# Modulation rows in four single buffers, multiplied behind a unit's last tap against a copy in PSUM, and feed-forward vectors loaded with the mixer's

## The chip, the cores and the metric

One core of a Trainium2 chip runs the whole program. The metric is the device time of one execution in microseconds (us); less is better. Engines are named as in the profile: PE (matmuls), PEld (its weight loads), DVE (vector), ACT (scalar), POOL (GpSimd), SP (the queue that issues most transfers).

## The reference, cut to what matters

256 tokens of width 1024 pass through two two-layer networks, one behind the other. The first has no modulation. The second modulates every layer with vectors that depend on the conditioning vector `c` alone:

```python
cond = jax.nn.silu(c)
for l in range(2):
    mod = cond @ ada_w[l] + ada_b[l]                 # 1024 -> 6 * 1024
    sh1, sc1, g1, sh2, sc2, g2 = split(mod, 6)
    h = rms_norm(x, norm1_g[l]) * (1 + sc1) + sh1
    x = x + g1 * (mixers(h) @ w_out[l])
    h = rms_norm(x, norm2_g[l]) * (1 + sc2) + sh2
    u = causal_dwconv(h @ ffn_up[l], ffn_conv[l], 3 taps) + ffn_conv_b[l]
    a, g = split(u, 2)
    x = x + g2 * ((a * silu(g)) @ ffn_down[l])
```

The feed-forward blocks of the first network are `(silu(h Wg) * (h Wu)) Wd`, without taps. All four feed-forward blocks have 2816 hidden columns.

## The kernel before, in words

The program runs eight stages: delta-rule mixer (g), feed-forward (f0), latent attention (a), feed-forward (f1), mixer (m0), feed-forward (f2), mixer (m1), feed-forward (f3). Every matmul with a weight is made of three products of high and low parts, so each weight chunk of 512 KB is loaded by SP (`weights`, L458), cast by ACT to its high part (L464), and its low part is made by DVE (L469) or POOL (L467), as a string per stage says. Chunks lie in seven or eight buffers, so this work runs ahead of PE.

A feed-forward block goes through 22 units of 128 hidden columns. Units 0 and 1 come out of `first_units`, token half by token half, with two accumulators of the pool `pa` (four PSUM banks, tag "acc"). From unit 2 on, `mm3_a` fills a `ps_gu` tile (four buffers). The element work of a unit in f0 and f1 is a SiLU on ACT (L735), a product on DVE (L736), a cast on ACT (L737) and a difference on POOL (L738). In f2 and f3 it is longer: ACT scales by the third tap (L2229) and DVE adds the two other taps, for both halves (L2231, four instructions), then SiLU (L2233), product (L2234, POOL), cast and difference. `proj_out` then multiplies by the down weights, chunk by chunk, into four `ps_o` tiles of the pool `pa`: for each chunk first token half 0, then token half 1.

The modulation is worked out beside f0, f1 and f2, as a matrix-vector product on DVE. `ada_cond` (L1363) broadcasts `c` to 128 partitions and takes its SiLU. The transposed modulation weights come in 48 pieces of 1 MB, each two rows of 1024 values per partition. `ada_load` (L1371) issues a piece from ACT's queue into one of two buffers `ada_raw`; `ada_step` (L1381) takes the piece held, loads the next one, and multiplies both rows with `ada_cond`, each in one DVE instruction that also sums it up (L1394). A block does 16 pieces: `ada_step` is called ahead of the element work of every odd unit (11 times) and in the down projection at chunks 1, 5, 9, 13, 17 (`ada_every`). f3 has none. The normed rows `xn` of the block's start lie in the same two buffers, each taking a whole 2 x 1024 buffer for one row of 1024.

The taps and their bias in f2 and f3 (`f2s`, 176 values per partition) are loaded by SP at the start of the block (L2204), among the first weight chunks. `mix2` loads its own vectors (`lay`, L1428) behind the last weight load of the block before.

The order of the instructions on each engine is made at build time by a list scheduler: it takes the code in the order written as priority, simulates the engines, and gives each engine the first instruction that it finds ready. On the chip each engine then keeps that order. `issue_after(ins)` forbids that an instruction of the same engine is put ahead of `ins`.

Of the kernel before, what the change touches and what calls it, by code (L numbers as in the profile page):

```python
# [20 lines left out]
D = 1024  # L21
# [358 lines left out]
class Prog:  # L380
    def __init__(self, ctx, tc, ap):
# [18 lines left out]
        self.ada_held = None  # L400
        self.behind = None
# [240 lines left out]
    def proj_steps(self, x, act, wap, nk, gate=None, order=None, each=None, last=None, out=None, hold=None):  # L642
        nc = self.nc
        tiles = lambda t: [a[:, k] for a in (t if isinstance(t, list) else [t]) for k in range(a.shape[1])]
# [63 lines left out]
    def ffn1(self, x, i):  # L708
        nc = self.nc
        with ExitStack() as st:  # L710
# [3 lines left out]
            xn = [fp.tile([128, 2, D], F32, name="xn", tag="ada_raw", bufs=2)[:, 0] for _ in range(2)]  # L714
# [9 lines left out]
            for m in range(NFF):  # L724
                if m < 2:
                    ps = first[m]
                else:
                    ps = self.pm.tile([128, 2, S], F32, name="ps_gu", tag="mm")
                    for j in range(2):
                        w = self.weights(self.ap[f"f_gu{i}"][2 * m + j], CW)  # L730
                        self.mm3_a(ps[:, j, :], w, KD, 128, 0, 128, hl)
                if m % 2:
                    self.ada_step(fp)
                t = fp.tile([128, S], F32, name="gu_t", tag="gu_t", bufs=2)
                nc.scalar.activation(t, ps[:, 0, :], AF.Silu)  # L735
                nc.vector.tensor_tensor(t, t, ps[:, 1, :], op=ALU.mult)  # L736
                nc.scalar.copy(ah[:, m, :], t)  # L737
                nc.gpsimd.tensor_tensor(al[:, m, :], t, ah[:, m, :].bitcast(F32), op=ALU.subtract)  # L738
# [624 lines left out]
    def ada_cond(self, pool):  # L1363

        nc = self.nc
        c = pool.tile([128, D], F32, name="ada_c", tag="ada_raw", bufs=2)
        self.cond = pool.tile([128, D], F32, name="ada_cond")
        nc.scalar.dma_start(c, self.ap["c"].partition_broadcast(128))
        nc.scalar.activation(self.cond, c, AF.Silu)

    def ada_load(self, pool):  # L1371

        if not self.ada_todo:
            return
        l, c = self.ada_todo.pop(0)
        raw = pool.tile([128, 2, D], F32, name="ada_raw", tag="ada_raw", bufs=2)
        with self.tc.issue_after(self.last_copy.ins):
            self.nc.scalar.dma_start(raw, self.ap[f"ada{l}"][c])
        self.ada_held = l, c, raw

    def ada_step(self, pool, last=False):  # L1381
# [7 lines left out]
        if c == 0:  # L1389
            self.mods[l] = self.xp.tile([128, 48], F32, name=f"mod{l}", tag="mod", bufs=2)  # L1390
        mod = self.mods[l]
        for j in range(2):
            i = 2 * c + j
            nc.vector.tensor_tensor_reduce(raw[:, j], raw[:, j], self.cond, 1.0, 0.0, op0=ALU.mult, op1=ALU.add, accum_out=mod[:, i : i + 1])  # L1394
        if c == 23:
            nc.vector.tensor_tensor(mod, mod, self.col(f"adab{l}", 0, 48), op=ALU.add)
# [3 lines left out]
    def mod_rows(self, l, pool):  # L1400

        nc = self.nc
        mod = self.mods[l]
# [20 lines left out]
    def mix2(self, x, l):  # L1424
        nc, tc, ap = self.nc, self.tc, self.ap
        self.lay = self.xp.tile([128, LAYER.n], F32, name=f"lay{l}", tag="lay")
        with tc.issue_after(self.last_raw.ins):
            nc.sync.dma_start(self.lay, ap[f"layer{l}"])  # L1428
        with ExitStack() as st:
# [768 lines left out]
    def ffn2(self, x, l, out):  # L2198
        nc, tc, ap = self.nc, self.tc, self.ap
        with tc.tile_pool(name=f"ffc{l}", bufs=1, reuse_waits="tile") as fp, ExitStack() as st:  # L2200
            self.psum(st)
            xn = [fp.tile([128, 2, D], F32, name="xn", tag="ada_raw", bufs=2)[:, 0] for _ in range(2)]
            sm = fp.tile([128, FFN2.n], F32, name="f2s")
            nc.sync.dma_start(sm, ap[f"ffn2_{l}"])  # L2204
# [8 lines left out]
            for m in range(NFF):  # L2213
# [10 lines left out]
                if m % 2:  # L2224
                    self.ada_step(fp)
                u = fp.tile([128, 2, S], F32, name="gu_u", tag="gu_u", bufs=2)
                for j in (1, 0):
                    q = NFF * j + m
                    nc.scalar.activation(u[:, j], ps[:, j], AF.Identity, scale=cw[:, 3 * q + 2 : 3 * q + 3], bias=cb[:, q : q + 1])  # L2229
                    for d in (1, 2):  # L2230
                        nc.vector.scalar_tensor_tensor(u[:, j, d:], ps[:, j, : S - d], cw[:, 3 * q + 2 - d : 3 * q + 3 - d], u[:, j, d:], op0=ALU.mult, op1=ALU.add)  # L2231
# [45 lines left out]
```

## Time and profile before

| | us |
|---|---|
| median of 3 runs | 1560.41 |
| lowest, highest | 1558.67, 1565.21 |
| the profiled execution, its own time | 1568.4 |
| span of the profiled execution (first to last instruction) | 1566.7 |
| PE busy | 1458.5 (93%) |
| DVE busy | 1114.1 (71%) |
| ACT busy | 811.6 (52%) |
| POOL busy | 662.0 (42%) |

The span is cut by its stages. The four feed-forward blocks are alike in what PE does, so they can be laid side by side: the start (first normed rows and the two first units), the stretch of the other twenty units, and the down projection. What PE waits for in a stretch is shown by its waits; PEclk is the clock that TensorE was granted, as a share of full speed.

### The profile page before, as it was taken

What the parts mean: (1) busy time and instruction counts of PE and PEld (TensorE: products, weight loads), DVE (VectorE), ACT (ScalarE), POOL (GpSimd) and SP (SyncE); (2) the same over time, 40 slices, a digit from 0 to 9 for tenths busy, and PEclk for the clock granted to TensorE, in tenths of its full rate; (3) what the DMA queues carried; (4) which work ended last, traced back from release to release, by engine and by line L of the source; (5) the groups of instructions that cost most, each with busy time, mean ns of one, the idle gap of its engine ahead of it and who ended that gap; (6) DMA issues with size and microseconds to landing.
All of it is one profiled execution on the core that took longest, in us unless ns stands there. A gap on an engine that the chain in (4) does not pass through costs nothing. (4 is left out here: it accounts for less than half of the span.)

```text
span 1566.7 us, 25783 instructions
## 1 busy us (share of the span) xinstructions
PE 1458.5 (93%) x9586; PEld 1287.5 (82%) x9586; DVE 1114.1 (71%) x2350; ACT 811.6 (52%) x1476; POOL 662.0 (42%) x435
## 2 busy tenths in 40 slices
PE   5999989899999899999998989898999898899998
PEld 4998878699987787999887766898988676689987
DVE  3588668778675576888477587788966868766652
ACT  4676545544543564454355664555545465466651
POOL 3577623246452431533136322465534612236530
PEclk9999999999999999999999999999999999899999
DMA  4756622677883455898544325677764432465551
GB/s 159 232 165 188 187 69 66 209 288 282 297 312 107 152 176 188 304 329 315 178 131 133 108 68 168 226 273 264 265 235 142 129 108 68 142 213 186 191 188 39
DMA packets 103246, 292.96 MB, mean 187 GB/s; under 512 B 28072, under 2 KB 37968, under 8 KB 96976
## 3 DMA queue, kind: packets, MB, share of 16 engines
q1 hardware_dynamic: 93872, 237.12, 46.0%
q10 hardware_dynamic: 8896, 53.14, 9.3%
q8 instruction: 75, 1.23, 0.3%
q0 software_dynamic: 352, 1.06, 0.2%
q14 instruction: 51, 0.42, 0.1%
HBM read 288.04 MB, written 3.24 MB: 186 GB/s over the span
## 5 line engine op out<-in xcount | busy, mean ns | idle before, releaser
L467 POOL TENSOR_TENSOR wl<-raw,wh 128x1024 fp32r<-128x1024 f32 (+4 forms) x162 | 402.1, 2489 | 417.1 <-ACT wh L464 363.8
L464 ACT CAST wh<-raw 128x1024 fp32r<-128x1024 f32 (+3 forms) x421 | 423.2, 1018 | 235.7 <-PE ps_o L493 98.8
L469 DVE TENSOR_TENSOR wl<-raw,wh 128x1024 fp32r<-128x1024 f32 (+2 forms) x259 | 352.7, 1370 | 125.6 <-ACT wh L464 123.7
L480 PE MATMUL ps_gu<-h_hi,wh 128*128 128x256 f32 x1280 | 314.7, 283 | 5.5 <-DVE gu_u L2231 5.4
L480 PE MATMUL ps_gu<-h_lo,wh 128*128 128x256 f32 x1280 | 314.1, 283 | 0.0
L480 PEld LDWEIGHTS ps_gu<-h_hi,wh 128*128 128x128 f32 x1280 | 244.6, 191 | 6.3 <-issue 6.2
L480 PEld LDWEIGHTS ps_gu<-h_lo,wh 128*128 128x128 f32 x1280 | 244.6, 191 | 0.2
L1394 DVE CUSTOM_DVE_ANT_0 ada_raw<-ada_raw,ada_cond 128x1024 f32<-128x1024 f32 x96 | 166.2, 1746 | 63.8 <-DMA ada_raw<-in_ada 56.4
L483 PE MATMUL ps_gu<-h_hi,wl 128*128 128x256 f32 x1280 | 179.7, 283 | 3.5 <-POOL wl L467 3.5
L483 PEld LDWEIGHTS ps_gu<-h_hi,wl 128*128 128x128 f32 x1280 | 164.9, 191 | 4.1 <-POOL wl L467 3.9
L493 PE MATMUL ps_o<-wh,act_l 128*128 128x512 f32 x352 | 139.1, 395 | 0.0
L494 PE MATMUL ps_o<-wl,act_h 128*128 128x512 f32 x352 | 139.0, 395 | 0.0
L492 PE MATMUL ps_o<-wh,act_h 128*128 128x512 f32 x352 | 138.5, 393 | 0.0
L2231 DVE SCALAR_TENSOR_TENSOR gu_u<-ps_gu,f2s,gu_u 128x254 f32<-128x254 f32 (+1 forms) x176 | 81.5, 477 | 42.8 <-ACT gu_u L2229 40.8
L738 POOL TENSOR_TENSOR act_l<-gu_t,act_h 128x256 fp32r<-128x256 f32 x44 | 54.6, 1242 | 106.0 <-ACT act_h L737 106.0
L2234 POOL TENSOR_TENSOR gu_t<-gu_t,gu_u 128x256 f32<-128x256 f32 x44 | 49.9, 1133 | 90.0 <-DVE gu_u L2231 84.5
L494 PEld LDWEIGHTS ps_o<-wl,act_h 128*128 128x128 f32 x352 | 66.1, 188 | 15.6 <-issue 0.5
L492 PEld LDWEIGHTS ps_o<-wh,act_h 128*128 128x128 f32 x352 | 66.1, 188 | 15.4 <-issue 0.2
L493 PEld LDWEIGHTS ps_o<-wh,act_l 128*128 128x128 f32 x352 | 66.1, 188 | 15.2 <-issue 0.2
L737 ACT CAST act_h<-gu_t 128x256 fp32r<-128x256 f32 x44 | 17.7, 407 | 106.5 <-DVE gu_t L736 106.3
L2235 ACT CAST act_h<-gu_t 128x256 fp32r<-128x256 f32 x44 | 17.9, 407 | 97.3 <-POOL gu_t L2234 97.0
L480 PE MATMUL ps_g<-h_hi,wh 128*128 128x256 f32 x256 | 66.4, 294 | 0.0
(665 smaller groups left out, 3020.5 us busy)
## 6 DMA issues: line engine op xcount, KB each, us to landing
ada_raw<-in_ada ACTq DMA_DIRECT2D x48, 1024.0 KB, 6.0
raw<-in_f_gu SPq DMA_DIRECT2D x88, 512.0 KB, 5.0
raw<-in_u_gu SPq DMA_DIRECT2D x88, 512.0 KB, 4.3
raw<-in_f_dn SPq DMA_DIRECT2D x44, 512.0 KB, 5.4
raw<-in_u_dn SPq DMA_DIRECT2D x44, 512.0 KB, 4.4
raw<-in_g_qkv SPq DMA_DIRECT2D x32, 512.0 KB, 3.5
raw<-in_g_z SPq DMA_DIRECT2D x16, 512.0 KB, 4.3
raw<-in_g_out SPq DMA_DIRECT2D x16, 512.0 KB, 4.2
```

The costliest lines, as they stand in the source:

```text
L464: self.last_copy = nc.scalar.copy(wh[:, :cols], raw[:, :cols])
L467: nc.gpsimd.tensor_tensor(wl[:, :cols], raw[:, :cols], wh[:, :cols].bitcast(F32), op=ALU.subtract)
L469: nc.vector.tensor_tensor(wl[:, :cols], raw[:, :cols], wh[:, :cols].bitcast(F32), op=ALU.subtract)
L480: nc.tensor.matmul(ps, wh[:, k * width + m0 : k * width + m0 + m], xx[:, k, :], start=(n == 0), stop=(n == last))
L483: self.last_mm = nc.tensor.matmul(ps, wl[:, k * width + m0 : k * width + m0 + m], xh[:, k, :], start=False, stop=(n == last))
L492: nc.tensor.matmul(ps, xh, wh[:, sl], start=start, stop=False, **kw)
L493: nc.tensor.matmul(ps, xl, wh[:, sl], start=False, stop=False, **kw)
L494: nc.tensor.matmul(ps, xh, wl[:, sl], start=False, stop=stop, **kw)
L738: nc.gpsimd.tensor_tensor(al[:, m, :], t, ah[:, m, :].bitcast(F32), op=ALU.subtract)
L1394: nc.vector.tensor_tensor_reduce(raw[:, j], raw[:, j], self.cond, 1.0, 0.0, op0=ALU.mult, op1=ALU.add, accum_out=mod[:, i : i + 1])
L2231: nc.vector.scalar_tensor_tensor(u[:, j, d:], ps[:, j, : S - d], cw[:, 3 * q + 2 - d : 3 * q + 3 - d], u[:, j, d:], op0=ALU.mult, op1=ALU.add)
L2234: nc.gpsimd.tensor_tensor(t, t, u[:, 0], op=ALU.mult)
```

## The change

Five things are changed.

1. `ada_raw` has four buffers of one row (512 KB) instead of two of two rows. A piece is two transfers of one row each. The normed rows `xn` take one such buffer each.
2. `ada_cond` copies its result into two further PSUM tiles of the pool `pa` (two ACT copies of 128x512), named `cond_ps`. While these are held, a row is multiplied in two halves of 512, each with one input from PSUM; the two sums lie in two columns that are added at the end. `proj_steps` drops them, so in the down projection the rows are multiplied whole with the SBUF copy, as before.
3. `ada_step` is written behind the unit's product (f0, f1) or its last tap (f2), and its multiplications are held behind that instruction on DVE.
4. `mods` has twice the columns, is cleared at its start, and one addition of 48 columns joins the halves.
5. The feed-forward vectors `f2s` lie in the pool `xp` and are loaded in `mix2`, behind `lay`.

```diff
     def proj_steps(self, x, act, wap, nk, gate=None, ...):
         nc = self.nc
+        self.cond_ps = None
...
-            xn = [fp.tile([128, 2, D], F32, name="xn", tag="ada_raw", bufs=2)[:, 0] for _ in range(2)]
+            xn = [fp.tile([128, D], F32, name="xn", tag="ada_raw", bufs=4) for _ in range(2)]
...
-                if m % 2:
-                    self.ada_step(fp)
                 t = fp.tile([128, S], F32, name="gu_t", tag="gu_t", bufs=2)
                 nc.scalar.activation(t, ps[:, 0, :], AF.Silu)
-                nc.vector.tensor_tensor(t, t, ps[:, 1, :], op=ALU.mult)
+                last_use = nc.vector.tensor_tensor(t, t, ps[:, 1, :], op=ALU.mult)
+                if m % 2:
+                    self.ada_step(fp, after=last_use)
...
     def ada_cond(self, pool):
-        c = pool.tile([128, D], F32, name="ada_c", tag="ada_raw", bufs=2)
+        c = pool.tile([128, D], F32, name="ada_c", tag="ada_raw", bufs=4)
...
+        self.cond_ps = [self.pa.tile([128, 512], F32, name="ps_cond", tag="acc") for _ in range(2)]
+        for i, ps in enumerate(self.cond_ps):
+            nc.scalar.copy(ps, self.cond[:, i * 512 : i * 512 + 512])
...
     def ada_load(self, pool):
-        raw = pool.tile([128, 2, D], F32, name="ada_raw", tag="ada_raw", bufs=2)
+        raw = [pool.tile([128, D], F32, name="ada_raw", tag="ada_raw", bufs=4) for _ in range(2)]
         with self.tc.issue_after(self.last_copy.ins):
-            self.nc.scalar.dma_start(raw, self.ap[f"ada{l}"][c])
+            for j in range(2):
+                self.nc.scalar.dma_start(raw[j], self.ap[f"ada{l}"][c][:, j])
...
         for j in range(2):
             i = 2 * c + j
-            nc.vector.tensor_tensor_reduce(raw[:, j], raw[:, j], self.cond, 1.0, 0.0, op0=ALU.mult, op1=ALU.add, accum_out=mod[:, i : i + 1])
+            for half, cond in enumerate(self.cond_ps or [self.cond]):
+                r = raw[j][:, half * 512 : half * 512 + 512] if self.cond_ps else raw[j]
+                with self.tc.issue_after(after.ins) if after else ExitStack():
+                    nc.vector.tensor_tensor_reduce(r, r, cond, 1.0, 0.0, op0=ALU.mult, op1=ALU.add, accum_out=mod[:, half, i : i + 1])
         if c == 23:
-            nc.vector.tensor_tensor(mod, mod, self.col(f"adab{l}", 0, 48), op=ALU.add)
+            nc.vector.tensor_tensor(mod[:, 0], mod[:, 0], mod[:, 1], op=ALU.add)
+            nc.vector.tensor_tensor(mod[:, 0], mod[:, 0], self.col(f"adab{l}", 0, 48), op=ALU.add)
...
         with tc.issue_after(self.last_raw.ins):
             nc.sync.dma_start(self.lay, ap[f"layer{l}"])
+            self.f2s = self.xp.tile([128, FFN2.n], F32, name=f"f2s{l}", tag="f2s")
+            nc.sync.dma_start(self.f2s, ap[f"ffn2_{l}"])
...
-            sm = fp.tile([128, FFN2.n], F32, name="f2s")
-            nc.sync.dma_start(sm, ap[f"ffn2_{l}"])
+            sm = self.f2s
...
-                if m % 2:
-                    self.ada_step(fp)
                 u = fp.tile([128, 2, S], F32, name="gu_u", tag="gu_u", bufs=2)
                 for j in (1, 0):
...
                     for d in (1, 2):
-                        nc.vector.scalar_tensor_tensor(u[:, j, d:], ps[:, j, : S - d], ...)
+                        last_use = nc.vector.scalar_tensor_tensor(u[:, j, d:], ps[:, j, : S - d], ...)
+                if m % 2:
+                    self.ada_step(fp, after=last_use)
```

## Rows read from the trace of the kernel before

**Rows 1.** Busy time by stretch; stretches are those of the feed-forward blocks (x: instructions)

```profile
core 0: us, PE busy (x) PEld busy (x) DVE busy (x) ACT busy (x) POOL busy (x), PEclk, DMA share, GB/s
323.80:439.20 115.40, 115.40 (x965) 115.40 (x964) 90.73 (x96) 53.48 (x83) 66.37 (x36) 1.00 0.80 293
...
616.30:730.20 113.90, 113.90 (x965) 113.90 (x964) 97.01 (x114) 56.54 (x86) 51.77 (x30) 1.00 0.86 312
730.20:793.00 62.80, 62.80 (x269) 50.23 (x268) 36.52 (x50) 23.01 (x33) 13.35 (x9) 1.00 0.59 201
971.90:991.70 19.80, 16.19 (x73) 12.54 (x71) 9.11 (x14) 7.36 (x10) 0.20 (x1) 0.91 0.80 293
991.70:1120.60 128.90, 119.93 (x964) 118.64 (x963) 118.71 (x157) 72.30 (x120) 77.42 (x50) 0.96 0.71 254
...
1387.60:1501.70 114.10, 114.10 (x965) 113.93 (x964) 77.27 (x117) 76.16 (x126) 64.22 (x48) 1.00 0.57 186
```

**Rows 2.** PE waits (total us, times, longest): 971.9 to 991.7, then 991.7 to 1120.6

```profile
PE ps_gu L634 <- ACT first_raw L627: 3.0, 1, 3.0
...
PE ps_gu L480 <- DVE gu_u L2231: 5.4, 3, 4.8
PE ps_gu L483 <- POOL wl L467: 3.5, 2, 1.9
```

**Rows 3.** Busy time by stretch: two short stretches of the third block

```profile
1025.10:1028.50 3.40, 3.40 (x18) 3.40 (x18) 2.43 (x5) 2.54 (x5) 1.96 (x3) 0.51 0.90 349
1094.80:1100.20 5.40, 5.38 (x25) 5.40 (x26) 5.40 (x10) 4.48 (x7) 2.46 (x3) 0.50 0.93 342
```

**Rows 4.** Instructions by line: duration ns min/median/max, first and last start us

```profile
L1394 DVE CUSTOM_DVE_ANT_0 ada_raw<-ada_raw,ada_cond x96: 1210/1274/3445, 325.6 to 1152.8; 128x1024 f32<-128x1024 f32 x96
...
L2231 DVE SCALAR_TENSOR_TENSOR gu_u<-ps_gu,f2s,gu_u x176: 465/479/487, 994.4 to 1507.0; 128x255 f32<-128x255 f32 x88, 128x254 f32<-128x254 f32 x88
...
L669 DVE TENSOR_TENSOR x_t<-ps_o,x_t x16: 679/688/692, 293.4 to 794.1; 128x512 f32<-128x512 f32 x16
...
L595 DVE SCALAR_TENSOR_TENSOR xn<-x_t,rstd,row x24: 740/751/2830, 302.6 to 1373.0; 128x512 f32<-128x512 f32 x24
L595 DVE SCALAR_TENSOR_TENSOR xn<-ps_o,fn_r,row x4: 743/746/746, 795.4 to 805.3; 128x512 f32<-128x512 f32 x4
```

**Rows 5.** Timeline of the third block: start us, us, instruction [idle before <-releaser]

```profile
1080.29 0.34 ACTq L1378 DMA_DIRECT2D ada_raw<-in_ada  x1
...
1088.86 1.23 DVE L1394 CUSTOM_DVE_ANT_0 ada_raw<-ada_raw,ada_cond 128x1024 f32<-128x1024 f32 x1 [4.54 <-DMA ada_raw<-in_ada]
```

**Rows 6.** Timeline of the third block, 1014 to 1020 us

```profile
1014.54 0.74 POOL L2234 TENSOR_TENSOR gu_t<-gu_t,gu_u 128x256 f32<-128x256 f32 x1 [2.15 <-DVE gu_u L2231]
...
1016.69 3.00 DVE L1394 CUSTOM_DVE_ANT_0 ada_raw<-ada_raw,ada_cond 128x1024 f32<-128x1024 f32 x1
```

**Rows 7.** Timeline of ScalarE before the third block's first unit

```profile
973.55 0.36 ACTq L1368 DMA_DIRECT2D ada_c<-in_c  x1
...
980.64 1.28 ACT L1369 ACT_TABLE_LOAD   x1 [2.04 <-DMA ada_c<-in_c]
981.93 1.06 ACT L1369 ACTIVATE ada_cond<-ada_c 128x1024 f32<-128x1024 f32 x1
982.90 0.57 ACT L627 COPY first_raw<-ps_gt 128x512 f32<-128x512 f32 x1
```

**Rows 8.** Timeline: last vector step of unit 21 in the four blocks

```profile
445.64 0.41 DVE L736 TENSOR_TENSOR gu_t<-gu_t,ps_gu 128x256 f32<-128x256 f32 x1
...
734.59 0.41 DVE L736 TENSOR_TENSOR gu_t<-gu_t,ps_gu 128x256 f32<-128x256 f32 x1
...
1138.95 0.47 DVE L2231 SCALAR_TENSOR_TENSOR gu_u<-ps_gu,f2s,gu_u 128x254 f32<-128x254 f32 x1
...
1506.51 1.00 DVE L2231 SCALAR_TENSOR_TENSOR gu_u<-ps_gu,f2s,gu_u 128x255 f32<-128x255 f32 x2 [0.63 <-ACT gu_u L2229]
```

**Rows 9.** Instructions grouped, 991.7 to 1120.6: xcount | busy us, mean ns | idle before

```profile
L1394 DVE CUSTOM_DVE_ANT_0 ada_raw<-ada_raw,ada_cond 128x1024 f32<-128x1024 f32 x25 | 45.0, 1811 | 9.8 <-DMA ada_raw<-in_ada 9.8
```

More of the change, by code (lines that the diff above doesn't have):

```diff
@@ L643, in proj_steps @@
         nc = self.nc
+        self.cond_ps = None
         tiles = lambda t: [a[:, k] for a in (t if isinstance(t, list) else [t]) for k in range(a.shape[1])]
@@ L1375, in ada_load, with ada_step @@
         l, c = self.ada_todo.pop(0)
-        raw = pool.tile([128, 2, D], F32, name="ada_raw", tag="ada_raw", bufs=2)
+        raw = [pool.tile([128, D], F32, name="ada_raw", tag="ada_raw", bufs=4) for _ in range(2)]
         with self.tc.issue_after(self.last_copy.ins):
-            self.nc.scalar.dma_start(raw, self.ap[f"ada{l}"][c])
+            for j in range(2):
+                self.nc.scalar.dma_start(raw[j], self.ap[f"ada{l}"][c][:, j])
         self.ada_held = l, c, raw
-    def ada_step(self, pool, last=False):
+    def ada_step(self, pool, last=False, after=None):
         if not self.ada_held:
@@ L1389, in ada_step @@
         if c == 0:
-            self.mods[l] = self.xp.tile([128, 48], F32, name=f"mod{l}", tag="mod", bufs=2)
+            self.mods[l] = self.xp.tile([128, 2, 48], F32, name=f"mod{l}", tag="mod", bufs=2)
+            nc.vector.memset(self.mods[l], 0.0)
         mod = self.mods[l]
@@ L1402, in mod_rows @@
         nc = self.nc
-        mod = self.mods[l]
+        mod = self.mods[l][:, 0]
         c = pool.tile([128, 6, 8], F32, name="mod_c")
@@ L2201, in ffn2 @@
             self.psum(st)
-            xn = [fp.tile([128, 2, D], F32, name="xn", tag="ada_raw", bufs=2)[:, 0] for _ in range(2)]
-            sm = fp.tile([128, FFN2.n], F32, name="f2s")
-            nc.sync.dma_start(sm, ap[f"ffn2_{l}"])
+            xn = [fp.tile([128, D], F32, name="xn", tag="ada_raw", bufs=4) for _ in range(2)]
+            sm = self.f2s
             cw, cb = sm[:, 0:132], sm[:, 132:176]
@@ L2230, in ffn2 @@
                     for d in (1, 2):
-                        nc.vector.scalar_tensor_tensor(u[:, j, d:], ps[:, j, : S - d], cw[:, 3 * q + 2 - d : 3 * q + 3 - d], u[:, j, d:], op0=ALU.mult, op1=ALU.add)
+                        last_use = nc.vector.scalar_tensor_tensor(u[:, j, d:], ps[:, j, : S - d], cw[:, 3 * q + 2 - d : 3 * q + 3 - d], u[:, j, d:], op0=ALU.mult, op1=ALU.add)
+                if m % 2:
+                    self.ada_step(fp, after=last_use)
                 t = fp.tile([128, S], F32, name="gu_t", tag="gu_t", bufs=2)
```

## The prediction

> **What bounds the kernel now.** I read the share of busy time first: PE is busy 93% of the span, DVE 71%, ACT 52%, POOL 42%. So only time that PE stands still, or runs at its lower clock, can be won. Then I laid the same stretch of the four feed-forward blocks side by side [rows 1]: 20 units take 115.4 us in f0, 113.9 in f1, 128.9 in f2 and 114.1 in f3. PE is busy all through f0, f1 and f3, and idle for 9.0 us of f2 alone. f3 has the same taps as f2 and no modulation rows; f0 and f1 have the rows and no taps. Only both together cost something: 128.9 - 114.1 = 14.8 us.
>
> The waits of PE in that stretch name 8.9 of them: 5.4 us for a vector tap (L2231), of which one wait is 4.8, and 3.5 us for a low weight part made by POOL [rows 2]. [...]
>
> Why DVE is late shows in the timeline. The 4.8 us wait: DVE reached a modulation row whose transfer, issued at 1080.29, landed only at 1088.86, and stood idle for 4.54 us with taps behind it [rows 5]. The POOL waits: a row ran ahead of taps, POOL's product waited 2.15 us for them, and the next row took 3.00 us [rows 6]. A row takes 1.21 us at least and 3.45 at most [rows 4]; in f2's stretch 25 rows averaged 1.81 us and made 45.0 us of DVE [rows 9], out of 118.7 busy in 128.9 us [rows 1]. The stretching belongs to instructions with two SBUF inputs. The same line L595 takes 751 ns in the middle and up to 2830 with both inputs in SBUF, and 743 to 746 with one in PSUM; the taps (one input in PSUM) stay within 465 to 487 over 176 instructions [rows 4]. POOL works in 50 instructions of that stretch, and DVE and POOL hold each other up.
>
> The start of f2 has one more stall: ACT waits 2.04 us for the transfer of `c` (issued at 973.55), loads its table and does the SiLU, and only then copies the first unit's raw sums at 982.90 [rows 7]; PE waits 3.0 us for that copy [rows 2].
>
> **Part 1, rows from PSUM behind the taps.** The trace has no row product with a PSUM input. Its nearest row is the 128x512 sum of PSUM and SBUF, 688 ns [rows 4]: two halves are 1.38 us, against 1.21 for an undisturbed whole row and 1.81 for the mean one in f2. In f2 this moves DVE from 118.7 to 118.7 - 45.0 + 22 x 1.38 = 104 us of work in the stretch. Fewer rows (22, two per odd unit) fall into it, since they no longer run ahead. 104 of 114 us is 91%, more than f1's 97.0 of 113.9 (85%), where PE never waits.
> Order matters more than the sum. A tap is no longer behind a row of its own unit, and a row is asked for later; the next transfer needs the buffers of the piece two steps back, as before. Each piece is now two transfers, so ACT issues 48 more, at 0.34 us each [rows 5], some 16 us over three blocks. Behind a waiting issue stand the weight casts (L464) and ACT's element work; the cover is the chunks that were cast ahead, and ACT is busy 72 of 129 us in f2 [rows 1]. I put it at nothing; if the cover went, it would be a share of those 16 us.
> Ends: all of the excess goes, -14.8; or the late transfer stays, with its 4.8 us wait and the 2.7 us of slow clock behind it, -7.3. Since DVE stays fuller than in f1, I take -12. In f0 and f1 PE stands still nowhere in this stretch, so nothing is to be won: 0.
>
> [...]
>
> **Part 2, the start of a block.** `c` finds a free buffer and needn't wait for the first normed rows, so its transfer can go earlier. In return ACT does two copies of 128x512, about 0.57 us each by the raw-sum copy of that form [rows 7]. If `c` comes in time, f2 wins the 3.0 us wait and something of the slow clock behind it (0.91 over 19.8 us [rows 1]); I put that end at -4.2. If it doesn't, the two copies stand ahead of the raw sums: +1.2. I take -1.5 for f2. In f0 and f1 no PE wait hangs on ACT here; 0, with +1.2 each as the bad end.
>
> **Part 3, the added wait.** `cond_ps` holds two of the four accumulators, and the down projection wants all four. Two of its `ps_o` tiles now wait for the rows of unit 21, which stand behind that unit's last vector step. Before, that step ended 6.9 us after the stretch in f0 (446.05 against 439.20), 4.8 in f1, 18.8 in f2 and 5.8 in f3 [rows 8, 1]. With f2 like f3, and four halves of 0.69 us behind, the tiles come free 9.6, 7.6 and 8.6 us after PE could start. The cover is token half 0: 22 chunks take 62.8 us [rows 1], so one chunk 2.85 and its first half 1.43 us. Six chunks of first halves would hide it all. How many PE gets depends on the scheduler, which puts ready work first but reckons without DVE's stretching. Queued behind the wait are PE's own products, and the weight buffers that they would free. Ends: nothing (0), and 4 us in each block (+12); I take 1.5 each, +4.5, nearer to the good end since PE's order is made from what is ready.
>
> **Part 4, `f2s` and the rest.** In f2 and f3 SP issues one transfer less (about 0.4 us, by ACT's issue) among the first weight chunks, on which ACT waits; in the mixers it goes out behind `lay`, in the down projection before. -0.5, ends -1.6 and +0.5. The memset, the addition and the second sums are a few tenths of DVE; 0.
>
> **Sum.** -12 - 1.5 + 4.5 - 0.5 = -9.5 us. The profiled execution takes 1568.4 us (span 1566.7), so it would take 1558.9. It lies 8.0 us above the median of the runs shown; I take the same difference from the median: 1560.41 - 9.5 = 1550.9, say 1551.
>
> **The rivals.**
> A. *The accumulators bind, slower.* PE's order keeps token half 1 of the first chunk near the front, as written. Then PE has 1.43 us of work and waits about 8.2, 6.1 and 7.1 us at the three transitions, 21.4 us, and each wait is followed by slow clock like the 2.7 us behind the 4.8 us wait [rows 3], 8.1 us more: -12 - 1.5 - 0.5 + 29.5 = +15.5, 1576. For it: DVE runs behind PE at every block's end [rows 8]. Against it: the scheduler sees that the tiles are held. It turns the sign from about 14 us of waits on.
> B. *DVE stays the bound of f2, no change.* With 91% of DVE taken, and weight parts with two SBUF inputs still stretched by POOL, taps stay late: -4 there, 0 at the start, +2 at the transitions, -0.5: -2.5, 1558. For it: 85% hides and 92% doesn't [rows 1], and 91% lies nearer to the second. [...]
> C. *The order hardly changes*, since the scheduler already puts rows where it finds room: 0, 1560.
>
> **How the numbers follow.** Forecast 0.57, A 0.13, B 0.25, C 0.05. A change of less than 0.5% (7.8 us) can't be told from none here. The forecast's own range is -20 to -4: four fifths of it are faster by over 7.8 us (0.46), the rest is not. B gives 0.04 faster and 0.21 within, A 0.02 within and 0.11 slower, C 0.05 within. Together with rounding: faster 0.50, within 0.38, slower 0.12. The range takes the good ends of parts 1, 2 and 4 with no wait (-14.8 - 4.2 - 1.6, 1540) and on the other side B with four or five us of waits in some block (+6, 1567).
>
> **What would show it.** The 20 units of f2 at 115 to 118 us, and no wait of PE for a tap of several us; row halves of 0.65 to 0.75 us with hardly any spread; f0 and f1 unchanged at 114 to 116; the raw-sum copy of f2 about 2 us after the last product of its half. Wrong it is if `ps_o` products of PE wait for DVE row products at the blocks' ends for more than 4 us each, or if f2's stretch stays above 124 us, or if the mixers, which the change leaves alone, move by more than 3 us because the scheduler ordered them anew.

## The result

The change makes the kernel slower: 1581.59 us (median of 4 runs, 1578.24 to 1584.21) against 1561.41 for the kernel before, run beside it; the ratio is 1.0113, with a 95% interval of 1.0094 to 1.0132. The forecast was 1551 us. The profiled execution takes 1580.8 us (span 1578.7); that of before took 1568.4, 7 us above its own median, so the stages are also compared with a second profile of before (1563.3 us, run b0 below).

The stages, in us, cut at TensorE's first and last products of each (s: start of a block, u: its 20 units, d: its down projection; left out are f0's start, 18.9, 20.0 and 20.3 us, and the stages that did not move):

| | f0 d | f1 u | f1 d | f2 s | f2 u | f2 d | f3 s | f3 u |
|---|---|---|---|---|---|---|---|---|
| before, profile at hand | 61.8 | 114.0 | 62.6 | 19.8 | 129.0 | 62.8 | 19.1 | 114.2 |
| before, second profile | 61.8 | 114.0 | 62.6 | 19.7 | 130.3 | 62.8 | 16.7 | 114.2 |
| after | 65.9 | 120.8 | 68.0 | 14.1 | 117.2 | 78.3 | 14.9 | 115.6 |

The units of f2 won what was forecast (11.8 us, 13.1 against the second profile) and f2's start 5.7. The three down projections lost 4.1, 5.4 and 15.5 us, and f1's units 6.8: 31.8 together. With f3 (start -4.2, units +1.4) these stages make +11.5 us of the 12.0 between the two spans. Against the second profile they make +12.7 of 17.1; the rest lies in the mixer g and the attention a, which the change leaves alone (2.7 and 1.7 us longer).

The stretches of after, answering [rows 1] (us, PE busy with its count of instructions, then PEld, DVE, ACT, POOL, the granted clock, DMA):

```profile
440.20:506.10 65.90, 63.67 (x275) 51.44 (x274) 36.40 (x56) 23.28 (x30) 18.35 (x11) 0.97 0.59 204
622.50:743.30 120.80, 115.42 (x965) 115.25 (x964) 83.59 (x147) 58.80 (x88) 42.67 (x30) 0.99 0.83 286
743.30:811.30 68.00, 64.22 (x269) 50.99 (x268) 40.90 (x62) 24.15 (x34) 13.22 (x7) 0.97 0.58 202
...
1002.70:1119.90 117.20, 114.91 (x965) 114.21 (x964) 98.50 (x179) 73.89 (x122) 64.73 (x50) 1.00 0.79 269
1119.90:1198.20 78.30, 66.26 (x269) 51.89 (x269) 50.56 (x86) 28.35 (x40) 22.46 (x16) 0.91 0.66 222
```

Read the line of f2's units (1002.70) first. VectorE's busy time in f2's units fell from 118.7 to 98.5 us, and TensorE stands still there for 2.3 us where it was 9.0. Then the last: in f2's down projection TensorE is idle for 12.0 us, and its granted clock is 0.91. What it waits for, from f0's units to the end of block 2 (us in total, times, longest):

```profile
PE ps_o L493 <- DVE mod L1405: 9.6, 3, 3.8
PE ps_o L495 <- DVE wl L470: 8.0, 1, 8.0
...
PE ps_mr L1423 <- DVE mod_c L1421: 5.4, 1, 5.4
```

The first line is three waits of a `ps_o` product for a row product, one at each block's end: the wait on `cond_ps`, which the prediction had priced at 1.5 us each. The other two lines, a weight split and the transpose of the gathered sums, it had not named at all.

**f0, a held accumulator.** VectorE at the end of f0's units, in its own order:

```profile
437.91 1.23 DVE L1405 CUSTOM_DVE_ANT_0 ada_raw<-ada_raw,ada_cond 128x1024 f32<-128x1024 f32 x1 [3.93 <-DMA ada_raw<-in_ada]
...
440.53 1.76 DVE L1405 CUSTOM_DVE_ANT_0 ada_raw<-ada_raw,ada_cond 128x1024 f32<-128x1024 f32 x1
...
443.36 1.21 DVE L1405 CUSTOM_DVE_ANT_0 ada_raw<-ada_raw,ada_cond 128x1024 f32<-128x1024 f32 x1
...
444.50 0.41 DVE L736 TENSOR_TENSOR gu_t<-gu_t,ps_gu 128x256 f32<-128x256 f32 x1
444.84 0.68 DVE L1405 CUSTOM_DVE_ANT_0 ada_raw<-ada_raw,ps_cond 128x512 f32<-128x512 f32 x1
...
446.05 0.68 DVE L1405 CUSTOM_DVE_ANT_0 ada_raw<-ada_raw,ps_cond 128x512 f32<-128x512 f32 x1
```

and TensorE beside it:

```profile
444.17 0.39 PE L495 MATMUL ps_o<-wl,act_h 128*128 128x512 f32 x1
446.79 0.50 PE L493 MATMUL ps_o<-wh,act_h 128*128 128x512 f32 x1 [2.23 <-DVE mod L1405]
```

The first three rows are whole ones, against `ada_cond`: they belong to the *down projection*, whose steps have no `after`, and the order made at build time has put them ahead of unit 21's product (444.50) and the halves held behind it. The first of them stands 3.93 us for its transfer. TensorE had 18 products of token half 0, three chunks, and then waits until the third half at 446.05 has read the first of the two `ps_cond` tiles for the last time. In f1 the same picture costs 3.8 us, with two whole rows ahead that stand 3.28 and 3.05 us for their transfers. Behind the stop in f0, and behind those in f1's units and in f2 that follow below, TensorE has stretches with a granted clock of 0.50 to 0.54:

```profile
447.60:451.20 3.60, 3.60 (x10) 2.82 (x9) 1.33 (x3) 1.14 (x2) 0.00 (x0) 0.53 1.00 383
708.20:710.50 2.30, 2.30 (x12) 2.30 (x12) 0.00 (x0) 0.26 (x1) 0.00 (x0) 0.50 0.72 226
1142.00:1148.00 6.00, 6.00 (x15) 4.76 (x16) 4.42 (x7) 2.37 (x3) 2.01 (x3) 0.54 0.67 227
```

**f2, VectorE late by 20 us.** Here TensorE stops first for a weight split, then for the tile; with 0.4 us for a cast before them, 12.0 us in 14. VectorE's order, then TensorE's:

```profile
1132.41 1.23 DVE L1405 CUSTOM_DVE_ANT_0 ada_raw<-ada_raw,ada_cond 128x1024 f32<-128x1024 f32 x1 [5.56 <-DMA ada_raw<-in_ada]
...
1135.88 1.64 DVE L470 TENSOR_TENSOR wl<-raw,wh 128x1024 fp32r<-128x1024 f32 x1
...
1139.12 0.99 DVE L2242 SCALAR_TENSOR_TENSOR gu_u<-ps_gu,f2s,gu_u 128x255 f32<-128x255 f32 x2
1140.03 0.68 DVE L1405 CUSTOM_DVE_ANT_0 ada_raw<-ada_raw,ps_cond 128x512 f32<-128x512 f32 x1
```

```profile
1137.58 0.79 PE L495 MATMUL ps_o<-wl,act_h 128*128 128x512 f32 x1 [7.99 <-DVE wl L470]
1141.99 0.79 PE L493 MATMUL ps_o<-wh,act_h 128*128 128x512 f32 x1 [3.61 <-DVE mod L1405]
```

A whole row of the down projection holds VectorE for 5.56 us. Its buffer came free with unit 19's halves, at 1124.7, and its transfer was issued at 1126.13, because the issue stood on ScalarE behind a cast that waited for POOL:

```profile
1126.13 0.41 ACT L2248 CAST act_h<-gu_t 128x256 fp32r<-128x256 f32 x1 [3.15 <-POOL gu_t L2247]
1126.13 0.82 ACTq L1385 DMA_DIRECT2D ada_raw<-in_ada  x2
```

The split at 1135.88, which TensorE needs at 1129.6, stands behind that row. Unit 21's last tap ends at 1140.1, 20.2 us after the stretch of units (before: 18.8 [rows 8]).

**f1, a wait that was moved onto TensorE.** The step that ends a layer's vector falls into f1. VectorE sums, makes `mod_c`, and TensorE transposes it (L1423):

```profile
703.76 0.41 DVE L736 TENSOR_TENSOR gu_t<-gu_t,ps_gu 128x256 f32<-128x256 f32 x1
704.09 0.68 DVE L1405 CUSTOM_DVE_ANT_0 ada_raw<-ada_raw,ps_cond 128x512 f32<-128x512 f32 x1
...
707.50 0.16 DVE L1421 COPY mod_c<-mod 128x8 f32<-128x8 f32 x1
```

and TensorE:

```profile
707.81 0.38 PE L1423 MATMUL ps_mr<-ident,mod_c 128*48 128x128 f32 x1 [5.38 <-DVE mod_c L1421]
```

The step now begins behind the unit's product, and TensorE, whose order had the transpose right after that unit's matmuls, stands for 5.38 us.

### The profile page after: what moved, and what is told of

Read it like the earlier page. It is cut to its first block, busy times and chain, and to the rows that moved or that the text cites. A ratio compares the mean times of both kernels' runs of the same rounds, so it can differ in the third digit from the quotient of the medians.

```text
span 1578.7 us, 26025 instructions
## 1 busy us (share of the span) xinstructions
PE 1457.7 (92%) x9586; PEld 1286.6 (81%) x9586; DVE 1072.7 (68%) x2486; ACT 821.4 (52%) x1482; POOL 625.6 (40%) x435
## 4 chain that ended last, share of the span: by engine, by line
PE 30%; DVE 11%; ACT 4%; POOL 3%; DMA 3%; issue 2%; SPq 0%; ACTq 0%; POOLq 0%; DVEq 0%
PE ps_gu L481 5%; PE ps_o L493 4%; PE ps_o L494 4%; PE ps_o L495 4%; DVE wl L470 2%; PE ps_gu L484 2%; ACT wh L465 2%; POOL wl L468 1%; DVE gu_u L2242 1%; DMA raw<-in_u_gu 1%; DVE ada_raw L1405 1%; PE ps_bs L1993 1%; POOL gu_t L2247 1%; DMA raw<-in_w_d 1%; ACT gu_u L2240 0%
## 5 line engine op out<-in xcount | busy, mean ns | idle before, releaser
L468 POOL TENSOR_TENSOR wl<-raw,wh 128x1024 fp32r<-128x1024 f32 (+4 forms) x162 | 387.1, 2397 | 473.2 <-ACT wh L465 390.3
L470 DVE TENSOR_TENSOR wl<-raw,wh 128x1024 fp32r<-128x1024 f32 (+2 forms) x259 | 347.1, 1345 | 184.7 <-ACT wh L465 182.9
L740 POOL TENSOR_TENSOR act_l<-gu_t,act_h 128x256 fp32r<-128x256 f32 x44 | 45.1, 1027 | 107.7 <-ACT act_h L739 107.7
L1405 DVE CUSTOM_DVE_ANT_0 ada_raw<-ada_raw,ps_cond 128x512 f32<-128x512 f32 x132 | 82.6, 680 | 0.0
L2247 POOL TENSOR_TENSOR gu_t<-gu_t,gu_u 128x256 f32<-128x256 f32 x44 | 42.3, 963 | 75.6 <-DVE gu_u L2242 75.6
L481 PE MATMUL ps_g<-h_lo,wh 128*128 128x256 f32 x256 | 66.0, 292 | 0.0
L2240 ACT ACTIVATE gu_u<-ps_gu,f2s 128x256 f32<-128x256 f32 x88 | 49.2, 561 | 23.4 <-DVE gu_u L2242 21.1
```

Of the source, the lines that this page charges most:

```text
L468: nc.gpsimd.tensor_tensor(wl[:, :cols], raw[:, :cols], wh[:, :cols].bitcast(F32), op=ALU.subtract)
L470: nc.vector.tensor_tensor(wl[:, :cols], raw[:, :cols], wh[:, :cols].bitcast(F32), op=ALU.subtract)
L481: nc.tensor.matmul(ps, wh[:, k * width + m0 : k * width + m0 + m], xx[:, k, :], start=(n == 0), stop=(n == last))
L1405: nc.vector.tensor_tensor_reduce(r, r, cond, 1.0, 0.0, op0=ALU.mult, op1=ALU.add, accum_out=mod[:, half, i : i + 1])
L2247: nc.gpsimd.tensor_tensor(t, t, u[:, 0], op=ALU.mult)
```

## The experiments

Every run in one table: median, ratio to the kernel before with its interval, and the stages of its profiled execution as above.

| run | us | ratio (interval) | f0 d | f1 u | f1 d | f2 s | f2 u | f2 d |
|---|---|---|---|---|---|---|---|---|
| b0_before_again | 1563.5 | 1.0005 (0.9987 to 1.0022) | 61.8 | 114.0 | 62.6 | 19.7 | 130.3 | 62.8 |
| after | 1581.6 | 1.0113 (1.0094 to 1.0132) | 65.9 | 120.8 | 68.0 | 14.1 | 117.2 | 78.3 |
| e1_no_psum | 1577.0 | 1.0088 (1.0058 to 1.0118) | 61.8 | 122.5 | 62.6 | 14.1 | 125.4 | 73.9 |
| e2_no_hold | 1571.2 | 1.0051 (1.0026 to 1.0075) | 70.7 | 115.1 | 62.6 | 14.1 | 129.2 | 62.7 |
| e3_free_early | 1563.6 | 0.9995 (0.9979 to 1.0011) | 61.8 | 122.0 | 62.6 | 14.1 | 117.3 | 70.7 |
| e4_c23_free | 1557.9 | 0.9960 (0.9945 to 0.9975) | 61.8 | 114.7 | 62.6 | 14.1 | 117.1 | 71.4 |
| e5_down_held | 1553.3 | 0.9927 (0.9908 to 0.9945) | 61.8 | 114.7 | 62.6 | 14.1 | 117.1 | 69.8 |
| e6_only_down_held | 1565.6 | 1.0005 (0.9990 to 1.0020) | 61.9 | 120.8 | 62.6 | 14.1 | 117.1 | 73.5 |
| e7_buffers_only | 1573.0 | 1.0051 (1.0030 to 1.0072) | 63.7 | 115.2 | 62.6 | 14.1 | 134.6 | 62.7 |
| e8_free_at_19 | 1558.8 | 0.9966 (0.9951 to 0.9980) | 61.8 | 114.7 | 62.6 | 14.1 | 117.4 | 72.8 |
| e9_vectors_early | 1564.6 | 1.0006 (0.9987 to 1.0024) | 61.9 | 114.0 | 62.6 | 15.3 | 132.4 | 62.7 |
| e10_two_steps_moved | 1551.9 | 0.9924 (0.9906 to 0.9943) | 61.8 | 114.7 | 62.6 | 14.1 | 117.6 | 65.2 |
| e11_one_step_moved | 1556.1 | 0.9942 (0.9924 to 0.9960) | 61.8 | 114.7 | 62.6 | 14.1 | 117.1 | 69.3 |

**The kernel before, again.** It is there for a second profile.

> The kernel before once more, to see what its profile shows in another execution. If the 4.8 us wait of PE for a tap and the slow clock behind it belong to every execution, the 20 units of f2 take about 129 us again. If they came from one late transfer in one execution, the stretch is about 121 us (129 less 4.8 and 2.7), and the profiled execution lies near the median of 1561 instead of 8 us above it. Then only about 7 of the 14.8 us that I counted as excess were there to be won.

f2's units take 130.3 us, with tap waits of 8.0 us, the longest 6.1. So the excess of 14.8 us, from which the prediction started, is no accident of one late transfer.

**Which of the two parts gains, which loses.** e1 takes the PSUM copies out of the change and keeps the place; e2 keeps them and drops the hold:

```diff
-        self.cond_ps = [self.pa.tile([128, 512], F32, name="ps_cond", tag="acc") for _ in range(2)]
-        for i, ps in enumerate(self.cond_ps):
-            nc.scalar.copy(ps, self.cond[:, i * 512 : i * 512 + 512])
```

```diff
-                    self.ada_step(fp, after=last_use)
+                    self.ada_step(fp)
```

> The changed kernel without the two PSUM copies: rows are multiplied whole with the SBUF copy, still behind the unit's last vector step; buffers and early vectors stay. Theory H (the copies hold two of four accumulators into the down projection): no PE product waits for a row any more, the down projections of f0 and f1 are back at 62 and 63 us and that of f2 falls by 5 us or more: 1581.6 - 4 - 5 - 5 = 1567. Theory P (the place behind the last vector step is what costs, the accumulators only show it): the wait of 5.4 us for the gathered rows in f1 and the 8.0 us wait for a weight part in f2 stay: 1575 or more.

> The changed kernel with PSUM copies, but rows not held behind the last vector step (still written there): the scheduler may put them as early as their transfer allows, as in the kernel before. Theory H alone: the copies are still held by the rows of unit 21; if these run early, the accumulators come free early, so the waits shrink but need not vanish: 1562 to 1572. Theory P: f1's 5.4 us wait for the gathered rows goes, the 20 units of f1 are back at 114 us, and all three transitions heal: 1558 to 1563.

What TensorE waits for in f2's units, without the copies (total us, times, longest):

```profile
PE ps_gu L481 <- DVE gu_u L2239: 5.1, 5, 1.3
PE ps_gu L484 <- DVE wl L470: 3.4, 3, 2.6
```

and without the hold:

```profile
PE ps_gu L481 <- DVE gu_u L2242: 5.9, 3, 2.8
...
PE ps_gu L484 <- POOL wl L468: 1.8, 3, 1.1
```

Neither part alone heals f2's units: 125.4 with the hold alone, 129.2 with the copies alone, 117.2 with both. Held whole rows are stretched (e1's 96 take 1603 ns in the middle and up to 3423, against a shortest of 1210), and rows not held wait for transfers with other work of VectorE's behind them (112.9 us in 46 waits over e2, 25.5 in 10 over the change). On the loss both theories miss: without copies f0's and f1's down projections are at 61.8 and 62.6 again, as H says, yet the total stays at 1577.0, as P says, since f1's units (122.5) and f2's down projection (73.9) are lost by the place alone. e2 is at 1571 where P said 1558 to 1563: two whole rows of the down projection in f0 hold VectorE for 5.38 and 4.61 us there, and TensorE waits 5.8 us for a split behind them. The total lies in H's range, but no `ps_o` product waits for a row there.

**Give the copies up one step sooner.**

```diff
+                if m == 21:
+                    self.cond_ps = None
                 if m % 2:
                     self.ada_step(fp, after=last_use)
```

> The changed kernel, but the rows of unit 21 are multiplied whole with the SBUF copy, still held behind the last vector step: the PSUM copies come free two units earlier. Theory H: no PE product waits for a row at the start of a down projection: -4 in f0, -5 in f1, -4 or more in f2, 1568; f1's wait of 5.4 us and f2's wait of 8.0 us for a weight part stay. Theory P: the waits only move to another instruction behind DVE, and less than 5 us are won: 1577 or more.

1563.6, 18 us better than the change and better than either theory said. f0's and f1's down projections are back at 61.8 and 62.6, f2's goes from 78.3 to 70.7: 17.1 us in three stages. f1's units stay at 122.0.

**Let the last step go ahead, and hold the down projection's rows.** e4 is e3 with the first edit, e5 is e4 with the second, e6 is the change with the second alone (`unit_last` is the `after` of unit 21's step).

```diff
-                with self.tc.issue_after(after.ins) if after else ExitStack():
+                with self.tc.issue_after(after.ins) if after and c != 23 else ExitStack():
```

```diff
-        return lambda c: self.ada_step(pool, c == 17) if c % 4 == 1 and c < 18 else None
+        return lambda c: self.ada_step(pool, c == 17, self.unit_last) if c % 4 == 1 and c < 18 else None
```

> The changed kernel with the PSUM copies given up from unit 21 on (as in the run before it, 1563.6 us) and, besides, the step that ends a layer's vector (number 23 of the 24) not held behind the unit's last vector step. Theory O (what is left of the loss is the order in which engines that work in order stand at late transfers): in the up projection of feed-forward 1 that step's chain (row products, sums, mod_c, the transpose on TensorE) then runs ahead of the unit's product again, the 5.4 us wait of ps_mr for mod_c goes, and the stretch of 20 units falls from 122.0 to 114 to 116 us: about 1556.5 us. Theory K (what is lost in that stretch is the clock, and the wait a small part): the wait goes, the stretch stays above 119 us, about 1561 us. The down projection of feed-forward 2 stays near 70.7 us by both.

> The kernel before this one in the list with one more edit: the down projection's row products (steps 1, 5, 9, 13 and 17) also held behind the last vector step of unit 21. Theory O: no row product that waits for its transfer stands on VectorE ahead of unit 21's vector steps or of weight splits that its taps need; the first waits of the down projection's products of feed-forward 2 for VectorE (4.0 us for the tile's row products, and for a split) go or fall below 2 us, and that stretch falls from 70.7 to 62.5 to 65 us: about 1550 us. Theory L (the rows are late since the held products free their buffers late, and something waits for them wherever they stand): the stretch stays above 68 us, with waits for weight splits in place of those for the rows, and the time stays within 3 us of the run before.

> The changed kernel with a single edit, the down projection's row products held behind the last vector step of unit 21; PSUM copies kept until the down projection, as in the change. It prices the overtaking by itself. Theory O: the down projections of feed-forward 0, 1 and 2 fall from 65.9, 68.0 and 78.3 us to within 2 us of 61.8, 62.6 and 65: 1581.6 less 4, 5 and 13 is about 1560 us. Theory H (the hold of the accumulators counts by itself): the held halves alone, some 5 of 0.68 us behind unit 20's and 21's vector steps, keep token half 1's products waiting by 1 to 4 us in each; 1568 to 1575 us.

e4 does what theory O said: f1's units fall from 122.0 to 114.7 us, TensorE's wait for `mod_c` from 5.4 us to 0.4, and the total by 5.7 to 1557.9. That wait, clock included, is worth the 7 us.

e6 keeps the accumulators held and heals f0 and f1 all the same (61.9 and 62.6). With e3 this means that neither the held tiles nor the rows that overtake cost anything there by themselves: the halves that hold the tiles stood behind rows that stood behind transfers, and either edit cuts the chain. In f2 the held tiles do cost: the down projection takes 73.5 us, with a single wait,

```profile
PE ps_o L493 <- DVE mod L1406: 7.7, 1, 7.7
```

Holding the down projection's rows alone gives 1565.6, between O's 1560 and H's range.

In e5 theory O failed for f2: the down projection takes 69.8 us, not 62.5 to 65, so the stretch goes as L said, though not by the waits for splits that L named (see below). The total, 1553.3, is nearer to O's, but the stages don't say why: 1.6 us came from f2's down projection, and the mixer g, which the edit doesn't touch, is 2.3 us shorter in that profile. VectorE at f2's end in e5:

```profile
1104.18 0.47 DVE L2245 SCALAR_TENSOR_TENSOR gu_u<-ps_gu,f2s,gu_u 128x254 f32<-128x254 f32 x1
1104.57 0.67 DVE L1408 CUSTOM_DVE_ANT_0 ada_raw<-ada_raw,ps_cond 128x512 f32<-128x512 f32 x1
...
1106.39 0.68 DVE L1408 CUSTOM_DVE_ANT_0 ada_raw<-ada_raw,ps_cond 128x512 f32<-128x512 f32 x1
```

and all that TensorE waits for in that down projection:

```profile
PE ps_o L493 <- DVE mod L1408: 4.0, 1, 4.0
```

No row waits for a transfer here, and still unit 19's halves run from 1104.57 on, where TensorE had ended unit 21 at 1101.0. Is it the tile they hold, or VectorE's lateness?

**Give the copies up two steps sooner.** e5 with `m == 19` for `m == 21`.

> The kernel with the down projection's rows held (1553.3 us) and one further edit: the PSUM copies are given up two units sooner, from the step of unit 19 on, so that the rows of units 19 and 21 are whole ones against the SBUF tile. In the profile of the run before, the down projection of feed-forward 2 (69.8 us) has a single gap of 4.4 us, ended by the row halves of unit 19, which stand on VectorE behind unit 19's last vector step 3.6 us after TensorE could start, and 13 products at 420 ns behind it. Theory H (a held accumulator is what is left): gap and slow products go, the stretch falls to 62.5 to 64 us and the total to 1546 to 1548 us. Theory D (VectorE is simply late there, and whole rows make it later): a gap of 3 us or more stays, then ended by a weight split or by unit 21's last vector step; the stretch stays above 68 us, or the two more whole rows per block lengthen the 20 units of feed-forward 2 from 117.1 to 120 us or more; total 1552 to 1556 us.

Theory D: the gap does not go, it changes its name. TensorE's longest wait in f2's down projection is now

```profile
PE ps_o L495 <- DVE wl L470: 6.8, 1, 6.8
```

and the rows of unit 19, now whole, take 3.03 and 1.75 us of VectorE among the taps:

```profile
1109.59 3.03 DVE L1408 CUSTOM_DVE_ANT_0 ada_raw<-ada_raw,ada_cond 128x1024 f32<-128x1024 f32 x1
...
1112.55 1.75 DVE L1408 CUSTOM_DVE_ANT_0 ada_raw<-ada_raw,ada_cond 128x1024 f32<-128x1024 f32 x1
```

The total, 1558.8, is even above D's 1552 to 1556.

**Take rows out of the last units.** e10 leaves out the steps of units 19 and 21 and does seven in the down projection for five; e11 leaves out unit 21's alone and does six. Both have step 23 not held, the down projection's rows held, and the copies kept as in the change.

```diff
-                if m % 2:
+                if m < 19 and m % 2:
                     self.ada_step(fp, after=last_use)
...
-        return lambda c: self.ada_step(pool, c == 17) if c % 4 == 1 and c < 18 else None
+        return lambda c: self.ada_step(pool, c == 19, self.unit_last) if c % 3 == 1 and c < 20 else None
```

> The changed kernel with step 23 not held, without the steps of units 19 and 21 in each block's up projection, and with seven steps in the down projection for five (every third of its units, from the second on; whole rows, held behind unit 21's last vector step). In the three runs before it VectorE was 3.6 us or more behind TensorE at the end of feed-forward 2's units whatever was done with the accumulators: its order there has the rows of two steps, the taps and the first splits of the down projection's weights. Theory D (that lateness is the loss): with 8 row halves (5.4 us) taken out of those units, the first products of the down projection wait under 1.5 us, that stretch falls from 69.8 to 63 to 65 us (28 us of whole rows then stand beside 63 us of products), units 117 us: about 1548 us. Theory S (VectorE's sum over block 2 binds, wherever the rows stand): the 28 us of whole rows make splits late in the down projection, it stays at 68 us or more, total 1553 to 1558 us.

> The same with only unit 21's step moved: six steps in the down projection, unit 19's step left with PSUM copies. Theory D: unit 19's halves still free the two PSUM tiles some 2 to 4 us late, so one gap of that size stays in feed-forward 2 and its down projection takes 66 to 69 us: about 1551 us. Theory S: 1553 to 1558 us, as for the other.

All of TensorE's waits in f2's down projection in e10:

```profile
PE ps_mr L1423 <- DVE mod_c L1421: 1.5, 1, 1.5
PE ps_o L495 <- DVE wl L470: 0.6, 1, 0.6
```

the stretch itself:

```profile
1100.60:1165.90 65.30, 63.22 (x270) 50.05 (x269) 51.15 (x78) 28.39 (x41) 24.06 (x16) 1.00 0.76 267
```

and in e11 the gap that was forecast for it:

```profile
PE ps_o L493 <- DVE mod L1405: 4.0, 1, 4.0
```

65.2 and 69.3 us, at the upper ends of theory D (63 to 65, 66 to 69), with VectorE's busy time in e10 as large as in the change (51.15 against 50.56 us): the sum of the work did not bind, its place in the queue did. Theory S, 68 us or more, falls by e10's stretch. The totals say less: 1551.9 and 1556.1 lie 4 and 5 us above what D gave, and the second within S's 1553 to 1558. e10 and e5 are 0.76% and 0.73% faster than the kernel before, with intervals that lie clear of 1.

**What the start of f2 is worth.** e7 keeps the four buffers, the early load and the later place in the text, without copies and hold; e9 is the kernel before with the early load alone:

```diff
             nc.sync.dma_start(self.lay, ap[f"layer{l}"])
+            self.f2s = self.xp.tile([128, FFN2.n], F32, name=f"f2s{l}", tag="f2s")
+            nc.sync.dma_start(self.f2s, ap[f"ffn2_{l}"])
```

> The kernel before with the four single-row buffers, the sums in two columns and the vectors loaded early, but neither PSUM copies nor the hold (the step only stands later in the program's text). It tells what gained 5.7 us at the start of feed-forward 2 and some 3 us at that of feed-forward 3. If it is the buffers and the early load: the two starts stay at 14.1 and 15 to 16 us, the 20 units of feed-forward 2 go back to 128 to 131, and the total is 1554 to 1558 us. If those starts were gained by the place of the rows behind the taps, they go back to 19.7 and 17 to 19 us and the total is 1562 to 1566 us.

> The kernel before with nothing changed but the load of the feed-forward's vectors at the start of the layer. If that load gained the 5.7 us at the start of feed-forward 2 (19.7 to 14.1 us) and some 1 to 4 us at that of feed-forward 3: both starts shorten here as well, total 1555 to 1559 us. If the four single buffers gained it (the broadcast of the conditioning vector has a buffer of its own, and no longer waits for one that the normalized tokens hold): the starts stay at 19 to 20 us and 16 to 19 us, total within 3 us of 1563.7 us.

In both the start shortens (14.1 us in e7 and 15.3 in e9, from 19.7), so the early load gains 4.4 of the 5.6 us by itself. And in neither does the total follow: 1573.0 and 1564.6, against 1554 to 1559 expected. The units take back what the start gave: start and units of f2 are 150.0 us in the second profile of before, 147.7 in e9 and 148.7 in e7. TensorE's waits in e9's units:

```profile
PE ps_gu L480 <- DVE gu_u L2232: 8.3, 3, 3.9
PE ps_gu L483 <- POOL wl L467: 2.4, 2, 1.9
```

VectorE is busy for 121.5 of the 132.3 us there (118.7 of 128.9 in [rows 1]); that it sets the pace of these units, so that TensorE only reaches its waits sooner, is the author's estimate from these numbers. By their medians e7 is 8.4 us slower than e9, with intervals that lie apart. They differ by the four single buffers, the sums in two columns and the later place in the text. e7's profiled execution (1564.7) is its fastest of ten, so its stages leave unsaid where its other runs lose these 8 us; which of the three costs them, and whether the change pays them too, no run shows.

## Why the prediction was wrong, point by point

- **Part 1, f2's units: right.** -12 was forecast, measured -11.8 (-13.1 against the second profile). 98.5 us of VectorE against a forecast 104: of the 22 rows that were reckoned into the stretch only 18 (36 halves, 24.5 us) ran there, and the four of units 19 and 21 fell behind its end, where Part 3 pays for them. The halves last 671 to 689 ns over 132 instructions (681 in the middle), as the 688 ns row suggested, with hardly any spread; they start 0.61 us apart, so that a row costs 1.22 us of VectorE from start to start, where an undisturbed whole one costs 1.14 (443.36 to 444.50 in f0). The two halves are so 0.08 us dearer than the whole row from start to start. POOL's part in the stretching can be counted in the trace of before: each of the 45 rows that took over a quarter longer than the shortest had a POOL instruction beside it, and the 30 rows without one took 1210 to 1228 ns; POOL's twelve splits (L467) in f2's units averaged 2982 ns, its eight in f3's, where VectorE has no rows, 2411. That it "belongs to instructions with two SBUF inputs" is too narrow: `rs_s` (L509) and `mx` (L1321), with one SBUF input, took up to 2262 and 2321 ns against shortest ones of 147 and 151, again with POOL beside them. The place of the halves was as necessary as their price: the hold alone (e1) keeps about a third of the gain, the copies alone (e2) none or 1 us.
- **Part 1, f0 and f1 at 0: wrong for f1, +6.8.** "PE stands still nowhere in this stretch, so nothing is to be won" was read as "nothing is to be lost". The moved step issues more than row products: the 24th ends in a transpose on TensorE, and with it a wait of VectorE's became one of TensorE's. e4 shows it: 7.3 us back by letting that one step go ahead.
- **Part 1, the order on VectorE.** "a row is asked for later; the next transfer needs the buffers of the piece two steps back, as before" was written down and not followed up: a held row frees its buffer later too. In f2 the buffers of unit 19 came free from 1124.7 on, the next piece was issued at 1126.13, after 1.4 us behind ScalarE's cast, and landed at 1132.4, where VectorE already stood.
- **Part 2, the start: -1.5 forecast, -5.7 measured**, beyond the end of -4.2. The wait for the raw sums went altogether. Most of it is the early load, which the prediction had put at -0.5 under Part 4 (e9), and without the healed units it is worth nothing in the total (1.0006). f3's units are 1.4 us longer after the change, and as much in e9, so the early load costs that much there; why stayed open.
- **Part 3, the added wait: the step that failed, +4.5 forecast, +25.0 measured** (4.1, 5.4 and 15.5). The tiles were reckoned free 9.6, 7.6 and 8.6 us after TensorE could start; the second one was so after 7.1, 9.2 and 22.6 (the first 0.6 sooner). In f0 and f1 the delay is about what was reckoned, and the cover was too short: three chunks of token half 0 in f0, 4.3 us, where the prediction asked for six. In f2 the error is "With f2 like f3": the 18.8 us of [rows 8] were taken for a result of the late rows that Part 1 heals. The lag stayed, at 20.2. By itself it had cost nothing (f2's down projection took 62.8 us before, and takes 65.2 in e10 with unit 21's last tap still 13.6 us behind); it costs what TensorE must wait for behind it, here a split and two tiles. TensorE stopped there first for a split 8.0 us late, a wait that the prediction had no line for.
- **What was not in the sum:** the five steps of the down projection. The diff gives them no `after`, and so they alone could go ahead, with their transfers still under way, while all other rows were held. e6 prices that: the three down projections take 198.0 us with those rows held, 212.2 in the change and 187.2 before.
- **The rivals.** A had the sign and nearly the size (+15.5, 1576), the size partly by luck: it reckoned tile waits of 8.2, 6.1 and 7.1 us, which were 2.2, 3.8 and 3.6, and the split in f2 and f1's units, which it did not have, filled the sum up. In f0 and f1 the loss came by its mechanism, a tile held while TensorE has too little of token half 0, with the slow clock behind it (0.53 over 3.6 us in f0, 0.50 over 3.0 in f1); e6 adds that without overtaking rows the held tile costs nothing there. It too took f2's end at 8.6 us. Its 8.1 us of slow clock are three times the 2.7 of Part 1, half of the 5.4 us at 0.50 in [rows 3], and no row shows that half of such a stretch is lost; the trace of after shows 128x512 products 0.43 us apart at a clock of 0.50 (752.50 to 754.20) and 0.23 at 1.00 (744.00 to 747.50), so that by estimate the stretches of 3.6, 3.0 and 6.0 us behind the three transitions lost some 5.5 us. Its chance, 0.13, was too low: "the scheduler sees that the tiles are held" is true of the order, and the order is fixed before a transfer is late. B did not arise: VectorE came down to 84% in f2's units (98.5 of 117.2), not 91%, about f1's share (85%), at which TensorE waited for nothing in that stretch of before.
- **What would show it.** Of the signs of a right step 1 those in f2 came (units at 117.2 us, no tap wait above 0.2, halves of 0.68 us, the raw-sum copy directly behind its half's last product); "f0 and f1 unchanged at 114 to 116" did not, since f1's units took 120.8. None of the signs of a wrong forecast came as written: `ps_o` waited for row products 2.2, 3.8 and 3.6 us, where 4 was the mark, f2's stretch stayed under 124, and the mixers moved by under 2 us against the profile at hand, and by 2.7 at most against the second. The marks watched single waits; three middling ones with slow clock behind them, a split and a transpose made the loss.

## What to carry to other kernels

The hold of an instruction on VectorE had three bills here: the buffers it freed later (free from 1124.7, the next transfer landed at 1132.4), the instructions of the same kind that were *not* held and overtook it (three down projections of 212.2 us, 198.0 once those rows were held too), and another engine that ended its chain (TensorE's 5.38 us for `mod_c`); write down all three before pricing a hold. In f2 VectorE's last tap lay 18.8 us behind the end of TensorE's units, and the cut waits in the middle did not shorten that lag (20.2 after): look at what the first engine will wait for behind such a lag, and move work out of that place, as e10 did (65.2 us for 78.3). And price an earlier start of a stage together with the stage: e9's start of f2 was 4.4 us shorter, its units 2.1 us longer than in the second profile of before, and the total the same (ratio 1.0006).

## What the runs showed of the hardware

- A row product with one input in PSUM has hardly any spread (671 to 689 ns, 132 of them), where the same operation on two SBUF inputs takes 1210 to 3431 ns for twice the length in the same execution. POOL beside it makes no difference to the halves: the 15 with no POOL instruction beside them took 674 to 687 ns, the 92 with one for over half their time 671 to 687. Of before's whole rows the 30 with none took 1210 to 1228 ns, the 51 with one for over half their time 1211 to 3445 (1755 in the middle).
- TensorE's stops of 2.2 us in f0, 5.4 in f1's units, 3.8 in f1's down projection and 8.0 and 3.6 in f2 were followed by 2 to 6 us at 0.50 to 0.54 of the clock. Not every stop of such a length was: behind one of 2.45 us in the same execution (until 814.6) the granted clock is 1.00 for 3 us, and e1's stretch from 1002.0 to 1127.6, nearly all of it f2's units, has 1.00 as a whole with stops of up to 2.6 us in it. A stop of 2.2 us in f0 made its stage 4.1 us longer, one of 5.4 in f1 6.8.
- Stages still differ between executions where no run changes them: the mixer g takes 300.7 to 305.0 us in these fourteen profiles, f0's start 18.9 and 20.0 in the two of the kernel before. Two spans can therefore be compared to some 4 us; stages in which TensorE hardly waits agree to some tenths (f0's units 115.4 to 115.6 us, f3's down projection 60.6 in all).
